# A two-layer mLSTM and RG-LRU trunk on one core: scores and gate inputs taken in wider products, row factors and gate logs moved by DMA

## The chip, the cores and the metric

One NeuronCore of a Trainium2 chip runs the whole kernel. The metric is the device time of one execution in microseconds. The engines are named as the profile names them: PE (matrix products; PEld is its weight load), DVE (vector), ACT (scalar, activations), POOL (GpSimd, which also issues DMAs of its queue) and SP (which issues most other DMAs).

## What is computed

`x` is 256 tokens by 2048 channels in float32, and there are two layers. Each layer does this, and a root-mean-square norm follows the last:

```python
u = rms_norm(x, norm_g);  p = u @ w_in          # w_in: 2048 x 12304
qk, v, o, z_a, ig, fg, xb, z_b = split(p)
q, k = split(silu(causal_dwconv(qk, qk_conv)))   # 8 heads of 128; k * 128**-0.5
i_pre = ig + i_bias;  log_f = log_sigmoid(fg + f_bias)      # 8 gate inputs each per token
h = mlstm(q, k, v, i_pre, log_f)                 # sum over s<=t of (q_t.k_s) exp(F_t-F_s+i_s-m_t) v_s
                                                 # divided by max(|the same sum of weights|, exp(-m_t))
h = layer_norm_per_head(h * sigmoid(o)) * head_norm_g
y_a = h * silu(z_a)
y_b = rg_lru(causal_dwconv(xb, lru_conv_w) + lru_conv_b, w_a, b_a, w_x, b_x, lam) * silu(z_b)
x = x + concat(y_a, y_b) @ w_out                 # w_out: 4096 x 2048
```

F is the running sum of log_f, and m the running maximum that keeps the exponentials bounded.

## The kernel before, in words

Every large product is made of three: a float32 value is split into a high part (rounded to the PE's input form) and a low part (the rest), and high by high, high by low and low by high are added in PSUM. The weights come in units of 1 MB (`raw`), in halves of 128x1024. For each half ACT casts the high part `wH` (L300), DVE subtracts to get the low part `wL` (`prepare`, L164 by its helper), and PE multiplies: 12 products of 128x128 by 128x512 (`mm_a`, L317 to L319). Four buffers each of `wH` and `wL` are in rotation, and splits are written out three halves ahead of the products (`AHEAD = 3`). Weights never stay: the program is one long stream of about 530 halves.

A layer handles four groups of two heads. A group takes the columns of qk, o, v, xb, z and zb in chunks of 8 halves each, the block-diagonal gates of the RG-LRU (`gate_half`, tile `ps_gt`) and the output products of the group before. All work on the results runs beside this stream as generators in a list `bg`. After each half `pump` gives them a budget (2.6, or 1.05 where at most two are waiting), and each `yield` takes its cost from it; `yield "wait"` lets the next generator go on, `yield None` ends the turn. `require` runs the generators until a key is set. The framework then schedules what was written for each engine, with the order as written as priority; an instruction can come well ahead of where it was written when its inputs are ready. An edge laid by hand (`order`, L208) keeps one instruction behind another.

The parts that the change touches:

- `rms_bcast` (L374). The norm factor `rstd` of each token lies with tokens on partitions. It is needed along the free axis on all partitions (`rb`). Two diagonal matrices `dg` are made on DVE from an identity, PE multiplies them by a matrix of ones (L380, `ps_rb`, plain float32), and DVE copies the result.
- `gates_mm` (L474). The 16 gate columns are laid out in a 128x104 weight `gwp` (high parts at columns 0 and 32, low parts at 64 and 96). For each of the 16 blocks of channels the high half of x (256 columns, L479) and the low half (L480) are multiplied in turn into the same 256 columns of `ps_g`.
- `gates_gen` (L483) multiplies rows of `ps_g` by `rb`, adds them, and makes the log of the forget gate, its running sum, and the running maximum on 8 partitions. `nG` goes to DRAM (L515, a POOL DMA), from where `e_gen` (L536) takes it to all partitions (`nb`, L539).
- `gates_tr` (L519) turns a 64x256 tile `sT` by two PE transposes (`ps_sT`, L527); DVE copies `aT` (L531), ACT makes `em`, the exponential (L532). `e_gen` needs `aT`, the denominators need `em`.
- In `qk_post` (L588) the scores of a head are six products by `mm3` (L560 to L562) into one bank `ps_S`: three of 256 columns and three of 128. DVE multiplies them by `E` into `Pt` in one instruction of 384 columns. Then P is split into `PH` and `PL`, and for each head and each half of the tokens P times v goes to `ps_n` (3 or 6 products of 258 columns); DVE makes denominator, `hh` and its statistics, and the turn may end after each.
- `aux` hands out the four PSUM banks that all these small products share.

Of the kernel before, what the change touches and what calls it, by code (L numbers as in the profile page):

```python
# [83 lines left out]
def tile_trunk(ctx, tc, x, xt, par, gw, gb, ws, final_g, out):  # L84
    nc = tc.nc
    V, S, G, PE = nc.vector, nc.scalar, nc.gpsimd, nc.tensor

    const = ctx.enter_context(tc.tile_pool(name="const", bufs=1))
# [64 lines left out]
    gbs = const.tile([NH, DEPTH, 2], F32, name="gbs")  # L153
    gwr = [small.tile([P, KT, 16], F32, tag="gwr", name=f"gwr{l}") for l in range(DEPTH)]

    ident = const.tile([P, P], F32, name="ident")
    make_identity(nc, ident)
    ones = const.tile([P, P], F32, name="ones")
    G.memset(ones, 1.0)
    epst = const.tile([P, 1], F32, name="epst")  # L160
    G.memset(epst, EPS)
# [46 lines left out]
    def order(ins, prev):  # L208
        tc.add_manual_dep(ins.ins, prev.ins.name,
                          mybir.DependencyInfo(mybir.DependencyClass.NoSync, mybir.DependencyReason.DATA),  # L210
                          reason="one table load for each group of functions")

    bg = deque()
    timed = []
# [89 lines left out]
    def mm_a(acc, aH, aL, k0, first, last, paired=False):  # L304
        def f(H, L):
            cols = "p (s k c) -> p k s c" if paired else "p (k c) -> p k c"
            Hv = H.rearrange(cols, k=2, **({"s": 2} if paired else {}))
            Lv = L.rearrange(cols, k=2, **({"s": 2} if paired else {}))
            a_H, a_L, ps = aH(), aL(), acc()
            for k in range(2):  # L310
                kt = k0 + k
                for t in range(2):
                    tsl = slice(P * t, P * t + P)
                    s = first and k == 0
                    e = last and k == 1
                    o = ps[:, t, :].rearrange("p (s c) -> p s c", s=2) if paired else ps[:, t, :]
                    PE.matmul(o, a_H[:, kt, tsl], Hv[:, k], start=s, stop=False)  # L317
                    PE.matmul(o, a_H[:, kt, tsl], Lv[:, k], start=False, stop=False)  # L318
                    PE.matmul(o, a_L[:, kt, tsl], Hv[:, k], start=False, stop=e)  # L319
        return f  # L320

    def mm_b(acc, k0, first, last):
# [42 lines left out]
    def rms_stats(l):  # L365
# [5 lines left out]
        V.reciprocal(out=rstd, in_=rstd)  # L371
        st["rstd", l] = rstd

    def rms_bcast(l):  # L374
        rstd = st["rstd", l]
        dg = work.tile([P, 2, P], F32, tag="sF", name="dg")
        for t in range(2):
            ts_(dg[:, t, :], ident, rstd[:, t : t + 1], ALU.mult)
        ps = aux("ps_rb")
        PE.matmul(ps[:, 0:T], ones, dg.rearrange("p t c -> p (t c)"), start=True, stop=True)  # L380
        rb = small.tile([P, T], F32, tag="rb", name="rb", bufs=1)
        V.tensor_copy(out=rb, in_=ps[:, 0:T])
        st["rb", l] = rb

    def new_ss():
# [87 lines left out]

    def gates_mm(l):  # L474
        ps = aux("ps_g")
        o = ps[0:104, 0:T]
        for kt in range(KT):
            gw_ = st["gwp"][kt // 8][:, kt % 8, :]
            PE.matmul(o, gw_, st["x"][:, kt, 0, :], start=kt == 0, stop=False)  # L479
            PE.matmul(o, gw_, st["x"][:, kt, 1, :], start=False, stop=kt == KT - 1)  # L480
        st["ps_g"] = ps

    def gates_gen(l):  # L483
        ps, rb = st["ps_g"], st["rb", l]

        scs = work.tile([P, 8, T], F32, tag="xcs", name="scs")

        def sc(nm):
            return scs[0:NH, "ifzsd".index(nm), :]

        gi, x_ = sc("i"), sc("f")
        t_ = sc("z")
        tt_(x_, ps[32:40, 0:T], rb[32:40, :], ALU.mult)
        tt_(t_, ps[96:104, 0:T], rb[96:104, :], ALU.mult)
        stt(x_, x_, gbs[:, l, 1:2], t_, ALU.add, ALU.add)
        t_ = sc("s")
        tt_(gi, ps[0:8, 0:T], rb[0:8, :], ALU.mult)
        tt_(t_, ps[64:72, 0:T], rb[64:72, :], ALU.mult)
        tt_(gi, gi, t_, ALU.add)
        yield 0.6  # L500
        q = log1p_exp_half(x_, sc)
        yield 4
        ts_(q, q, -2.0, ALU.mult)
        stt(x_, x_, 0.0, q, ALU.min, ALU.add)
        Fc = sc("z")
        V.tensor_tensor_scan(out=Fc, data0=ones[0:NH, 0:1].to_broadcast([NH, T]), data1=x_, initial=0.0, op0=ALU.mult, op1=ALU.add)
        sT = scs[0:64, 5, :]
        G.memset(sT, 0.0)
        stt(sT[0:8, :], gi, gbs[:, l, 0:1], Fc, ALU.add, ALU.subtract)
        Gm = sc("s")  # L510
        V.tensor_tensor_scan(out=Gm, data0=sT[0:8, :], data1=sT[0:8, :], initial=0.0, op0=ALU.max, op1=ALU.max)
        stt(sT[32:40, :], Fc, -1.0, Gm, ALU.mult, ALU.subtract)
        nG = sc("d")
        ts_(nG, Gm, -1.0, ALU.mult)
        nc.gpsimd.dma_start(out=nG_d[l], in_=nG)  # L515
        st["sT"] = sT
        yield 3

    def gates_tr(l):  # L519
        sT = st["sT"]  # L520
        yield None
        yield None
        for _ in range(2 + 2 * l):
            yield "wait"
        pt = aux("ps_sT")
        for t in range(2):
            PE.transpose(out=pt[:, 64 * t : 64 * t + 64], in_=sT[:, P * t : P * t + P], identity=ident[0:64, 0:64])  # L527
        ptv = pt[:, 0:128].rearrange("p (t c) -> p t c", t=2)
        aT = small.tile([P, 2, NH], F32, tag="aT", name="aT", bufs=1)
        em = small.tile([P, 2, NH], F32, tag="em", name="em", bufs=1)  # L530
        V.tensor_copy(out=aT, in_=ptv[:, :, 0:8])  # L531
        S.activation(out=em, in_=ptv[:, :, 32:40], func=AF.Exp)  # L532
        st["aT", l], st["em", l] = aT, em
        yield 0.3

    def e_gen(l, g):  # L536
        nb = small.tile([P, 2, T], F32, tag="nb", name="nb", bufs=1)
# [21 lines left out]
    def mm3(o, aH, aL, bH, bL, first=True, last=True):  # L559
        PE.matmul(o, aH, bH, start=first, stop=False)  # L560
        PE.matmul(o, aH, bL, start=False, stop=False)  # L561
        PE.matmul(o, aL, bH, start=False, stop=last)  # L562
# [25 lines left out]
    def qk_post(l, g, acc):  # L588
# [3 lines left out]
        def gen():  # L592
# [20 lines left out]
            E, em, so, (vH, vL) = st["E", l, g], st["em", l], st["so", l, g], st["v", l, g]  # L613
            Pt = work.tile([P, 2, 384], F32, tag="Pt", name="Pt")
            for h in range(2):
                ps = aux("ps_S")
                for o_, ss_, ts__ in ((0, slice(0, 128), slice(0, 256)), (256, slice(128, 256), slice(128, 256))):
                    mm3(ps[:, o_ : o_ + ts__.stop - ts__.start], q[:, 2 * h + 1, 0, ss_], q[:, 2 * h + 1, 1, ss_],
                        q[:, 2 * h, 0, ts__], q[:, 2 * h, 1, ts__])
                stt(Pt[:, h, :], ps[:, 0:384], DK_SCALE, E[:, h, :], ALU.mult, ALU.mult)  # L620
                yield 0.5
            PH = work.tile([P, 2, 384], F32R, tag="sD", name="PH")
            PL = work.tile([P, 2, 384], F32R, tag="sC", name="PL")
            S.copy(out=PH, in_=Pt)
# [4 lines left out]
            hh = work.tile([P, 2, 2, 256], F32, tag="sE", name="hh")  # L629
            mv = small.tile([P, 2, 2, 2], F32, tag="mv", name="mv", bufs=1)  # L630
            for h in range(2):
                for t in range(2):
                    pn = aux("ps_n")
                    o = pn[:, 0:258]
                    a = slice(P * t, P * t + P)
                    mm3(o, PH[:, h, a], PL[:, h, a], vH[:, 0, h, :], vL[:, 0, h, :], last=t == 0)
                    if t == 1:
                        mm3(o, PH[:, h, 256:384], PL[:, h, 256:384], vH[:, 1, h, :], vL[:, 1, h, :], first=False)
                    dn = small.tile([P, 1], F32, tag="dn", name="dn")
                    stt(dn, pn[:, 256:257], -1.0, em[:, t, 2 * g + h : 2 * g + h + 1], ALU.mult, ALU.max)  # L640
# [531 lines left out]
```

## Time and profile before

| | us |
|---|---|
| median of 3 runs (1498.24 to 1498.82) | 1498.77 |
| the profiled execution, its own time | 1498.6 |
| its span, first to last instruction | 1496.9 |
| PE busy in it | 1481.1 |
| DVE busy | 1053.3 |
| ACT busy | 916.0 |
| POOL busy | 79.2 |

Busy time counts each instruction from start to end; products overlap in the array, so the distance from one start to the next, called a slot here, says what a product costs in a dense stream. The granted TensorE clock is 0.998 of full speed on average over the span.

### The profile page before, as it was taken

The page shows a single profiled execution, that of the slowest core. Times are in us where ns is not written, and L with a number is a line of the kernel's source. Part 1 is how long each engine was busy: PE and PEld are TensorE (multiplying, and loading weights), DVE is VectorE, ACT ScalarE, POOL GpSimd, SP SyncE. Part 2 cuts the span into 40 slices and gives each one's busy share as a digit, 9 for nine tenths or more (in the row PEclk, how much of TensorE's full clock was granted, in tenths as well). Part 3 has the DMA queues.
Part 4 walks back from the last instruction along what each step waited for, and adds up shares of the span by engine and source line. Part 5 has one row for each costly group of instructions (what it writes and reads, how often), then busy time and mean ns, then how long its engine had stood idle before and what let it go on. Part 6 is the DMA issues. An engine that isn't in the chain of part 4 may idle for free.

```text
span 1496.9 us, 18541 instructions
## 1 busy us (share of the span) xinstructions
PE 1481.1 (99%) x6916; PEld 1239.3 (83%) x6916; DVE 1053.3 (70%) x1403; ACT 916.0 (61%) x1153; POOL 79.2 (5%) x138
## 2 busy tenths in 40 slices
PE   8999999999999999999999999999999999999997
PEld 6888888888888888888888888888888888888886
DVE  6777966676567855778867688766855678556794
ACT  6656855575456754558565667645855567555684
POOL 0001000000000000000000200000000000000002
PEclk9999999999999999999999999999999999999999
DMA  9766667766677666886775666568666776577773
GB/s 352 271 206 238 208 226 221 241 219 223 197 251 225 225 225 208 257 266 216 274 269 197 238 211 246 186 215 253 217 231 210 227 234 233 198 233 268 227 251 113
DMA packets 90074, 344.61 MB, mean 230 GB/s; under 512 B 9840, under 2 KB 29824, under 8 KB 67968
## 3 DMA queue, kind: packets, MB, share of 16 engines
q1 hardware_dynamic: 77888, 305.17, 58.7%
q0 software_dynamic: 9344, 33.58, 9.2%
q10 hardware_dynamic: 2752, 4.69, 0.9%
q8 instruction: 54, 0.88, 0.2%
q14 instruction: 36, 0.29, 0.1%
HBM read 306.68 MB, written 36.72 MB: 229 GB/s over the span
## 4 chain that ended last, share of the span: by engine, by line
PE 97%; DVE 1%; DMA 0%; ACT 0%; issue 0%; SPq 0%; DVEq 0%; ACTq 0%
PE acc L317 29%; PE acc L318 29%; PE acc L319 29%; PE ps_gt L724 3%; PE acc L332 3%; PE acc L955 1%; PE acc L954 1%; PE acc L956 1%; DMA raw<-in_ws_dram 0%; PE acc_x L954 0%; PE acc_x L955 0%; PE acc_x L956 0%; DVE wL L164 0%; PE ps_n L562 0%; PE ps_n L560 0%; PE ps_n L561 0%
## 5 line engine op out<-in xcount | busy, mean ns | idle before, releaser
L164 DVE TENSOR_TENSOR wL<-raw,wH 128x1024 fp32r<-128x1024 f32 (+1 forms) x526 | 636.9, 1217 | 340.3 <-ACT wH L300 340.0
L300 ACT CAST wH<-raw 128x1024 fp32r<-128x1024 f32 (+1 forms) x526 | 548.7, 1049 | 401.9 <-PE acc L319 369.8
L317 PE MATMUL acc<-wH,x_s 128*128 128x512 f32 x1472 | 574.3, 390 | 7.4 <-ACT wH L300 6.6
L318 PE MATMUL acc<-wL,x_s 128*128 128x512 f32 x1472 | 574.0, 390 | 0.4 <-DVE wL L164 0.4
L319 PE MATMUL acc<-wH,x_s 128*128 128x512 f32 x1472 | 573.2, 389 | 0.0
L317 PEld LDWEIGHTS acc<-wH,x_s 128*128 128x128 f32 x1472 | 276.7, 188 | 65.1 <-ACT wH L300 6.6
L318 PEld LDWEIGHTS acc<-wL,x_s 128*128 128x128 f32 x1472 | 276.7, 188 | 58.6 <-DVE wL L164 1.9
L319 PEld LDWEIGHTS acc<-wH,x_s 128*128 128x128 f32 x1472 | 276.7, 188 | 57.6
L317 PE MATMUL acc<-wH,yaH 128*128 128x512 f32 x224 | 87.8, 392 | 0.0
L319 PE MATMUL acc<-wH,ybL 128*128 128x512 f32 x224 | 87.4, 390 | 0.0
L319 PE MATMUL acc<-wH,yaL 128*128 128x512 f32 x224 | 87.3, 390 | 0.0
L317 PE MATMUL acc<-wH,ybH 128*128 128x512 f32 x224 | 87.2, 390 | 0.0
L318 PE MATMUL acc<-wL,ybH 128*128 128x512 f32 x224 | 87.2, 390 | 0.0
L318 PE MATMUL acc<-wL,yaH 128*128 128x512 f32 x224 | 87.2, 389 | 0.0
L429 POOL DMA_DIRECT2D fr<-moved x34 | 18.9, 555 | 724.2 <-DMA moved<-blk 426.7
L319 PEld LDWEIGHTS acc<-wH,ybL 128*128 128x128 f32 x224 | 42.0, 188 | 9.1 <-DVE ybL L164 0.3
L319 PEld LDWEIGHTS acc<-wH,yaL 128*128 128x128 f32 x224 | 42.0, 188 | 9.0
L318 PEld LDWEIGHTS acc<-wL,ybH 128*128 128x128 f32 x224 | 42.1, 188 | 8.4
L317 PEld LDWEIGHTS acc<-wH,ybH 128*128 128x128 f32 x224 | 42.0, 188 | 8.3
L318 PEld LDWEIGHTS acc<-wL,yaH 128*128 128x128 f32 x224 | 42.1, 188 | 8.2
L317 PEld LDWEIGHTS acc<-wH,yaH 128*128 128x128 f32 x224 | 42.1, 188 | 8.1
L425 DVE STREAM_TRANSPOSE blk<-tok 128x1024 f32<-128x1024 f32 x32 | 39.7, 1240 | 12.7 <-ACT tok L415 12.6
(208 smaller groups left out, 1387.5 us busy)
## 6 DMA issues: line engine op xcount, KB each, us to landing
raw<-in_ws_dram SPq DMA_DIRECT2D x172, 1024.0 KB, 5.0
raw<-in_ws_dram SPq DMA_DIRECT2D x182, 512.0 KB, 4.8
fr<-moved POOLq DMA_DIRECT2D x34, 512.0 KB, 5.8
moved<-blk SPq DMA_DIRECT2D x128, 128.0 KB, 2.3
x_d<-stage POOLq DMA_DIRECT2D x24, 512.0 KB, 5.4
x_d<-x_acc ACTq DMA_DIRECT2D x8, 512.0 KB, 7.2
x_acc<-x_d SPq DMA_DIRECT2D x8, 512.0 KB, 5.3
xp<-in_xt_dram SPq DMA_DIRECT2D x8, 256.0 KB, 7.0
```

What stands on the lines that cost most here:

```text
L164: return V.tensor_tensor(out=o, in0=a, in1=b, op=op)
L300: S.copy(out=H[:, o], in_=r[:, o])
L317: PE.matmul(o, a_H[:, kt, tsl], Hv[:, k], start=s, stop=False)
L318: PE.matmul(o, a_H[:, kt, tsl], Lv[:, k], start=False, stop=False)
L319: PE.matmul(o, a_L[:, kt, tsl], Hv[:, k], start=False, stop=e)
L332: PE.matmul(ps[:, ct, T * part : 2 * T], W[:, k, P * ct : P * ct + P], moving, start=first and k == 0 and part == 0, stop=last and k == 3 ...
L425: V.transpose(out=blk.rearrange("p m n -> p (m n)"), in_=tok.rearrange("p m c t j -> p (m c t j)"))
L429: G.dma_start(out=fr.rearrange("p a c t i -> p a (c t i)"), in_=moved)
L724: PE.matmul(o, W[:, ib, jl], xs[:, ib, a, :], start=j == 0 and i == 0 and W is Hv and a == 0, stop=i == 1 and W is Lv, skip_group_check=True)
L954: PE.matmul(o, yH[:, kt, tsl], Hv[:, k, cs], start=start and k == 0, stop=False)
L955: PE.matmul(o, yH[:, kt, tsl], Lv[:, k, cs], start=False, stop=False)
L956: PE.matmul(o, yL[:, kt, tsl], Hv[:, k, cs], start=False, stop=stop and k == 1)
```

## The change

In `gates_mm` high and low half of x are one product of 512 columns into two halves of the bank; DVE adds the halves afterwards. An edge puts the first of these products behind the last product that `mm_a` has written. The scores get a bank per block of 128 keys: one product takes high and low of q at once against the high part of k, a second adds low of k by high of q; DVE multiplies both halves by E (E is overwritten) and adds. P times v is written for both halves of the tokens of a head before the DVE work on either. The norm factor goes to DRAM and back to all partitions by two POOL DMAs, and `sT` is turned by a DVE transpose in blocks of 32x32 and eight POOL DMAs; the exponential and the key for E come two waits later. The identity and the matrix of ones go.

```diff
     def rms_bcast(l):
-        rstd = st["rstd", l]
-        dg = work.tile([P, 2, P], F32, tag="sF", name="dg")
-        for t in range(2):
-            ts_(dg[:, t, :], ident, rstd[:, t : t + 1], ALU.mult)
-        ps = aux("ps_rb")
-        PE.matmul(ps[:, 0:T], ones, dg.rearrange("p t c -> p (t c)"), start=True, stop=True)
         rb = small.tile([P, T], F32, tag="rb", name="rb", bufs=1)
-        V.tensor_copy(out=rb, in_=ps[:, 0:T])
+        G.dma_start(out=rb_d[l].rearrange("t p -> p t"), in_=st["rstd", l])
+        G.dma_start(out=rb, in_=rb_d[l].rearrange("t p -> (t p)").partition_broadcast(P))
...
     def gates_mm(l):
-            PE.matmul(o, gw_, st["x"][:, kt, 0, :], start=kt == 0, stop=False)
-            PE.matmul(o, gw_, st["x"][:, kt, 1, :], start=False, stop=kt == KT - 1)
+            m = PE.matmul(ps[0:104, :], st["gwp"][kt // 8][:, kt % 8, :], st["x"][:, kt].rearrange("p a t -> p (a t)"),
+                          start=kt == 0, stop=kt == KT - 1)
+            if kt == 0:
+                order(m, st["mm"])
...
     gates_gen:
-        tt_(x_, ps[32:40, 0:T], rb[32:40, :], ALU.mult)
+        tt_(x_, ps[32:40, T : 2 * T], rb[32:40, :], ALU.mult)
+        tt_(gi, ps[32:40, 0:T], rb[32:40, :], ALU.mult)
+        tt_(x_, x_, gi, ALU.add)
...
-        tt_(t_, ps[64:72, 0:T], rb[64:72, :], ALU.mult)
-        tt_(gi, gi, t_, ALU.add)
+        for rows, half in ((slice(0, 8), slice(T, 2 * T)), (slice(64, 72), slice(0, T))):
+            tt_(t_, ps[rows, half], rb[rows, :], ALU.mult)
+            tt_(gi, gi, t_, ALU.add)
...
     gates_tr:
-        pt = aux("ps_sT")
-        for t in range(2):
-            PE.transpose(out=pt[:, 64 * t : 64 * t + 64], in_=sT[:, P * t : P * t + P], identity=ident[0:64, 0:64])
-        V.tensor_copy(out=aT, in_=ptv[:, :, 0:8])
-        S.activation(out=em, in_=ptv[:, :, 32:40], func=AF.Exp)
+        V.transpose(out=sb, in_=sT)
+        for q_ in range(2):
+            for a in range(4):
+                rows = slice(32 * a, 32 * a + 32)
+                G.dma_start(out=at[q_][rows], in_=sv[32 * q_ : 32 * q_ + 32, :, a, 0:NH])
         yield 0.3
+        for _ in range(2):
+            yield "wait"
+        S.activation(out=at[1], in_=at[1], func=AF.Exp)
+        st["aT", l], st["em", l] = at
...
     scores, for h in range(2):
+                for b in range(2):
+                    n_ = T - P * b
+                    ps, ss_, ts__ = aux("ps_S"), slice(P * b, P * b + P), slice(P * b, T)
+                    both = ps[:, 0 : 2 * n_].rearrange("p (a t) -> p a t", a=2)
+                    PE.matmul(both, q[:, 2 * h + 1, 0, ss_], q[:, 2 * h, :, ts__], start=True, stop=False, ...)
+                    PE.matmul(ps[:, 0:n_], q[:, 2 * h + 1, 1, ss_], q[:, 2 * h, 0, ts__], start=False, stop=True, ...)
+                    stt(Pt[:, h, part], ps[:, n_ : 2 * n_], DK_SCALE, E[:, h, part], ALU.mult, ALU.mult)
+                    stt(E[:, h, part], ps[:, 0:n_], DK_SCALE, E[:, h, part], ALU.mult, ALU.mult)
+                tt_(Pt[:, h, :], Pt[:, h, :], E[:, h, :], ALU.add)
+                yield 1.0
...
     P times v, for h in range(2):
+                pns = []
                 for t in range(2):
-                    pn = aux("ps_n")
-                    o = pn[:, 0:258]
+                    pns.append(aux("ps_n"))
+                    o = pns[t][:, 0:258]
...
+                for t in range(2):
+                    pn = pns[t]
```

## Rows read from the trace of the kernel before

**Rows 1.** The page's first part: busy time, share of the span, count.
```profile
PE 1481.1 (99%) x6916; PEld 1239.3 (83%) x6916; DVE 1053.3 (70%) x1403; ACT 916.0 (61%) x1153; POOL 79.2 (5%) x138
```

**Rows 2.** Waits: who waited for whom, us in total, times, longest.
```profile
PE acc L317 <- DVE x_acc L164: 0.8, 1, 0.8
...
ACT wH L300 <- PE acc L319: 369.8, 263, 2.4
```

**Rows 3.** Timeline of PE, scores of a group: start us, us, engine, line, instruction.
```profile
111.15 0.39 PE L317 MATMUL acc<-wH,x_s 128*128 128x512 f32 x1
...
112.51 0.28 PE L560 MATMUL ps_S<-qks 128*128 128x256 f32 x1
...
112.87 0.23 PE L560 MATMUL ps_S<-qks 128*128 128x128 f32 x1
...
113.83 0.45 PE L317 MATMUL acc<-wH,x_s 128*128 128x512 f32 x1
114.11 0.39 PE L318 MATMUL acc<-wL,x_s 128*128 128x512 f32 x1
```

**Rows 4.** Timelines of DVE and PE: gate inputs in layer 0, norm factor in layer 1.
```profile
45.80 0.17 DVE L371 RECIPROCAL rstd<-rstd 128x2 f32<-128x2 f32 x1 [0.38 <-ACT rstd L370]
...
45.99 0.28 PE L479 MATMUL ps_g<-x_s,gwp 128*104 128x256 f32 x1
...
47.88 0.59 PE L380 MATMUL ps_rb<-dg,ones 128*128 128x256 f32 x2
...
793.15 0.40 PE L319 MATMUL acc<-wH,x_s 128*128 128x512 f32 x1
...
794.05 0.40 PE L318 MATMUL acc<-wL,x_s 128*128 128x512 f32 x1
```

**Rows 5.** Timeline of PE around the two transposes of layer 0.
```profile
73.29 0.39 PE L319 MATMUL acc<-wH,x_s 128*128 128x512 f32 x1
...
74.21 0.39 PE L318 MATMUL acc<-wL,x_s 128*128 128x512 f32 x1
```

**Rows 6.** Timeline of PE: 12 weight products behind a P piece, two such stretches.
```profile
129.66 0.39 PE L317 MATMUL acc<-wH,x_s 128*128 128x512 f32 x1
...
132.41 0.39 PE L317 MATMUL acc<-wH,x_s 128*128 128x512 f32 x1
...
232.27 0.40 PE L317 MATMUL acc<-wH,yaH 128*128 128x512 f32 x1
...
235.05 0.28 PE L560 MATMUL ps_n<-vH,PH 128*128 128x258 f32 x1
```

**Rows 7.** Timelines of POOL, DVE and ACT: gate logs until E, layer 0.
```profile
72.70 0.53 POOL L515 DMA_DIRECT2D nG_d<-scs  x1 [7.61 <-DVE scs L171]
...
82.15 1.01 DVE L172 TENSOR_SCALAR E<-nb,aT 128x256 f32<-128x256 f32 x4 [5.16 <-DMA nb<-nG_d]
...
83.19 0.85 ACT L551 ACTIVATE E<-E 128x768 f32<-128x768 f32 x1 [5.20 <-DVE E L172]
```

**Rows 8.** Timeline of PE, some five halves later.
```profile
95.87 0.39 PE L317 MATMUL acc<-wH,x_s 128*128 128x512 f32 x1
96.27 0.50 PE L318 MATMUL acc<-wL,x_s 128*128 128x512 f32 x1
```

**Rows 9.** Groups by line and form: busy us, mean ns of one, idle before.
```profile
L164 DVE TENSOR_TENSOR wL<-raw,wH 128x1024 fp32r<-128x1024 f32 x522 | 634.1, 1221 | 338.0 <-ACT wH L300 337.8
...
L300 ACT CAST wH<-raw 128x1024 fp32r<-128x1024 f32 x522 | 546.2, 1052 | 399.8 <-PE acc L319 369.8 <-DMA raw<-in_ws_dram 6.2 <-issue 5.2
...
L167 DVE SCALAR_TENSOR_TENSOR hh<-ps_n,dn,so 128x256 f32<-128x256 f32 x32 | 15.3, 479 | 0.3
...
L167 DVE SCALAR_TENSOR_TENSOR Pt<-ps_S,E 128x384 f32<-128x384 f32 x16 | 8.7, 545 | 5.6 <-PE ps_S L562 5.6
...
L164 DVE TENSOR_TENSOR scs<-ps_g,rb 8x256 f32<-8x256 f32 x8 | 3.3, 417 | 1.9 <-PE ps_g L480 1.8
```

**Rows 10.** DMA issues: engine, count, size, median us from issue to landing.
```profile
x_acc<-in_x_dram SPq DMA_DIRECT2D x4, 512.0 KB, 8.2
```

More of the change, by code (lines that the diff above doesn't have):

```diff
@@ L6 @@
 from concourse import mybir
-from concourse.masks import make_identity
 from concourse._compat import with_exitstack
@@ L154, in tile_trunk @@
     gwr = [small.tile([P, KT, 16], F32, tag="gwr", name=f"gwr{l}") for l in range(DEPTH)]
-    ident = const.tile([P, P], F32, name="ident")
-    make_identity(nc, ident)
-    ones = const.tile([P, P], F32, name="ones")
+    ones = const.tile([NH, 1], F32, name="ones")
     G.memset(ones, 1.0)
@@ L210, in order @@
                           mybir.DependencyInfo(mybir.DependencyClass.NoSync, mybir.DependencyReason.DATA),
-                          reason="one table load for each group of functions")
+                          reason="an order of the program")
     bg = deque()
@@ L318, in f @@
                     PE.matmul(o, a_H[:, kt, tsl], Lv[:, k], start=False, stop=False)
-                    PE.matmul(o, a_L[:, kt, tsl], Hv[:, k], start=False, stop=e)
+                    st["mm"] = PE.matmul(o, a_L[:, kt, tsl], Hv[:, k], start=False, stop=e)
         return f
@@ L372, in rms_stats @@
         st["rstd", l] = rstd
+    rb_d = [dram.tile([2, P], F32, name=f"rb_d{l}") for l in range(DEPTH)]
     def rms_bcast(l):
-        rstd = st["rstd", l]
-        dg = work.tile([P, 2, P], F32, tag="sF", name="dg")
-        for t in range(2):
-            ts_(dg[:, t, :], ident, rstd[:, t : t + 1], ALU.mult)
-        ps = aux("ps_rb")
-        PE.matmul(ps[:, 0:T], ones, dg.rearrange("p t c -> p (t c)"), start=True, stop=True)
         rb = small.tile([P, T], F32, tag="rb", name="rb", bufs=1)
-        V.tensor_copy(out=rb, in_=ps[:, 0:T])
+        G.dma_start(out=rb_d[l].rearrange("t p -> p t"), in_=st["rstd", l])
+        G.dma_start(out=rb, in_=rb_d[l].rearrange("t p -> (t p)").partition_broadcast(P))
         st["rb", l] = rb
@@ L475, in gates_mm @@
         ps = aux("ps_g")
-        o = ps[0:104, 0:T]
         for kt in range(KT):
-            gw_ = st["gwp"][kt // 8][:, kt % 8, :]
-            PE.matmul(o, gw_, st["x"][:, kt, 0, :], start=kt == 0, stop=False)
-            PE.matmul(o, gw_, st["x"][:, kt, 1, :], start=False, stop=kt == KT - 1)
+            m = PE.matmul(ps[0:104, :], st["gwp"][kt // 8][:, kt % 8, :], st["x"][:, kt].rearrange("p a t -> p (a t)"),
+                          start=kt == 0, stop=kt == KT - 1)
+            if kt == 0:
+                order(m, st["mm"])
         st["ps_g"] = ps
@@ L505, in gates_gen @@
         Fc = sc("z")
-        V.tensor_tensor_scan(out=Fc, data0=ones[0:NH, 0:1].to_broadcast([NH, T]), data1=x_, initial=0.0, op0=ALU.mult, op1=ALU.add)
+        V.tensor_tensor_scan(out=Fc, data0=ones.to_broadcast([NH, T]), data1=x_, initial=0.0, op0=ALU.mult, op1=ALU.add)
         sT = scs[0:64, 5, :]
@@ L515, in gates_gen @@
         nc.gpsimd.dma_start(out=nG_d[l], in_=nG)
-        st["sT"] = sT
+        st["sT"], st["sb"] = sT, scs[0:64, 6, :]
         yield 3
@@ L524, in gates_tr @@
             yield "wait"
-        pt = aux("ps_sT")
-        for t in range(2):
-            PE.transpose(out=pt[:, 64 * t : 64 * t + 64], in_=sT[:, P * t : P * t + P], identity=ident[0:64, 0:64])
-        ptv = pt[:, 0:128].rearrange("p (t c) -> p t c", t=2)
-        aT = small.tile([P, 2, NH], F32, tag="aT", name="aT", bufs=1)
-        em = small.tile([P, 2, NH], F32, tag="em", name="em", bufs=1)
-        V.tensor_copy(out=aT, in_=ptv[:, :, 0:8])
-        S.activation(out=em, in_=ptv[:, :, 32:40], func=AF.Exp)
-        st["aT", l], st["em", l] = aT, em
+        sb = st["sb"]
+        V.transpose(out=sb, in_=sT)
+        sv = sb.rearrange("p (t a i) -> p t a i", t=2, a=4)
+        at = [small.tile([P, 2, NH], F32, tag=f"at{q_}", name=f"at{q_}", bufs=1) for q_ in range(2)]
+        for q_ in range(2):
+            for a in range(4):
+                rows = slice(32 * a, 32 * a + 32)
+                G.dma_start(out=at[q_][rows], in_=sv[32 * q_ : 32 * q_ + 32, :, a, 0:NH])
         yield 0.3
+        for _ in range(2):
+            yield "wait"
+        S.activation(out=at[1], in_=at[1], func=AF.Exp)
+        st["aT", l], st["em", l] = at
     def e_gen(l, g):
@@ L615, in gen @@
             for h in range(2):
[L616 to L621, printed above, removed]
+                for b in range(2):
+                    n_ = T - P * b
+                    ps, ss_, ts__ = aux("ps_S"), slice(P * b, P * b + P), slice(P * b, T)
+                    both = ps[:, 0 : 2 * n_].rearrange("p (a t) -> p a t", a=2)
+                    PE.matmul(both, q[:, 2 * h + 1, 0, ss_], q[:, 2 * h, :, ts__], start=True, stop=False,
+                              skip_group_check=True)
+                    PE.matmul(ps[:, 0:n_], q[:, 2 * h + 1, 1, ss_], q[:, 2 * h, 0, ts__], start=False, stop=True,
+                              skip_group_check=True)
+                    part = slice(T * b, T * b + n_)
+                    stt(Pt[:, h, part], ps[:, n_ : 2 * n_], DK_SCALE, E[:, h, part], ALU.mult, ALU.mult)
+                    stt(E[:, h, part], ps[:, 0:n_], DK_SCALE, E[:, h, part], ALU.mult, ALU.mult)
+                tt_(Pt[:, h, :], Pt[:, h, :], E[:, h, :], ALU.add)
+                yield 1.0
             PH = work.tile([P, 2, 384], F32R, tag="sD", name="PH")
```

## The prediction

> **What bounds the kernel now.** I read the busy times first: PE is busy for 1481.1 of 1496.9 us, DVE for 70%, ACT for 61% [rows 1]. Busy alone proves little, so the waits come next. In the whole list PE waits for another engine's result behind its start only in a few places below 1 us; the largest is 0.8 us at the layer boundary [rows 2]. The other way round ACT waits 369.8 us, in 263 pieces, for PE to free a weight buffer [rows 2]. So this is a stream of products with everything else running ahead of it, and an edit is worth what it takes out of PE's dense sequence, less whatever new wait breaks through to PE.
>
> How far ahead is the rest? A split can start when PE has freed one of four buffers; PE then has three halves before it needs it. A half is 12 slots of 512 columns. Six of them, from 111.15 to 112.51, take 1.36 us [rows 3], so a slot is 0.227 and a half 2.72. Three halves are 8.2 us, cast and subtraction take 1.05 and 1.22 [rows 9], so ACT or DVE may stand still for about 5.9 us before PE stops. This is the cover on which everything below rests.
>
> **The change part by part.**
>
> *Scores.* From the first score product at 112.51 to the second weight product at 114.11 are 1.60 us; less one slot of 0.227 the 12 products of a group cost 1.373 [rows 3]. Three of 256 columns take 0.36 (112.51 to 112.87), 0.118 to 0.12 each; the remaining six of 128 columns take (1.373 - 6 x 0.118) / 6 = 0.111, nearly as much for half the columns. Their price is set by something per product, not by columns (there is a weight load with each). After: per head one of 512, two of 256, one of 128: 0.227 + 2 x 0.118 + 0.111 = 0.574, two heads 1.148. Saved 0.225 a group, eight groups 1.80 us. Bounds: the columns streamed are equal before and after (1152 a head), so if columns alone counted the saving would be 0; above, 12 x 0.12 - 1.148 would be 0.29 a group, 2.3.
>
> *Gate inputs.* 16 products of 256 columns take 1.89 us from 45.99 to 47.88 [rows 4], 0.118 each. 32 of them become 16 of 0.227: 3.78 - 3.63 = 0.15 a layer, 0.3 in all; between 0 and 0.3 by the same argument. The edge moves them behind one more half, on the same engine: nothing gained or lost there, since PE is dense on both sides.
>
> The Trainium skill, "TensorE: Matmul & The Clock Gate", section "Back-to-back issue gap", gives a warm product N/2.4 + 2.5 ns, which is 109 for 256 columns and 216 for 512 where the rows above show 118 and 227; by it the fixed part that merging saves is 2.5 ns, not 9. By the page the gate inputs would be worth an estimated 0.08 us instead of 0.3. I keep the rows.
>
> *Norm factor.* From 793.15 to 794.05 are 0.90 us with two weight slots in it [rows 4]: 0.45 for the two plain float32 products with their changeover. Twice: 0.9 us removed.
>
> *Transposes.* 73.29 to 74.21 is 0.92, less two slots: 0.466 [rows 5]. Twice 0.93. Both are nothing at the least only if other work had to fill PE there, and PE has weight products waiting in either place.
>
> *P products in one piece.* Their number and width stay. After a split piece the next 12 weight products take 2.78 us (232.27 to 235.05), after a joined one 2.75 (129.66 to 132.41), against 2.72 undisturbed [rows 6]. There are two changeovers fewer a group in six of eight groups (the first group of each layer already runs joined): at 0.03 each 0.4 us; between 0 and 0.7 (0.06 each).
>
> Sum: 1.80 + 0.30 + 0.90 + 0.93 + 0.40 = 4.3 us off PE.
>
> *What is added on DVE.* Per head four multiplications (two of 256 columns at 0.48 [rows 9], two of 128, at most the same) and a sum (as the 0.545 now) replace one of 0.545: at most 1.9 us more, 3.8 a group, 31 in all on an engine with 440 us free. In a group's score step this comes at once, and ACT waits with the cast of P behind it, with the casts of `wH` queued behind that on ACT. 3.8 is inside the 5.9, so I cost it at 0; without that cover it would be up to 3.8 a group. The gates get four more operations of 0.42 [rows 9], 1.7 us a layer, while copies and the diagonal go: 0.
>
> *The wait for rb.* Two DMAs in a chain now stand between `rstd` and the gate operations. The only such chain in the trace, `nG` to DRAM and back to `nb`, takes 9.45 us from issue at 72.70 to the first E at 82.15 [rows 7]. `rstd` is done at 45.97 [rows 4], so the factor is there at about 55.4. Gate products that start at 45.99 as now end at 49.6 (16 slots of 0.227); one half later, as the edge has it, at 52.3. DVE stands 3.1 to 5.8 us at its first gate operation, with splits `wL` queued behind it; against 5.9. Between 0 and, with six operations of 0.42 on top before the next split, 2.4 us of PE in a layer; I take 0, since the edge puts the need later.
>
> *The wait for the gate logs.* E now waits for `nb` until 82.15; DVE stands 5.16 us, ACT 5.20 behind it [rows 7]. This eats the cover: PE still loses 0.17 us at 95.87, where a slot takes 0.40 [rows 8]. After the change eight POOL issues of 0.53 [rows 7], 4.2 us, share the queue with `nb`, and an exponential on ACT waits for the last of them with `wH` casts queued behind it. If they go ahead of `nb`, `nb` lands about 1 us later than now; if behind, the last lands at 77.4 + 0.5 + 4.2 + 4.2 = 86.3 (half of the 9.45 chain a DMA), 4 us later. The need is written two halves, 5.4 us, later. So between -0.2 and +4 us a layer; I take +0.2 for both together, near the present loss, because the later need and the later landing about cancel.
>
> The Trainium skill, "DMA: Bandwidth & Descriptors", section "Anatomy of one DMA — SWDGE (gpsimd) path", gives a POOL DMA about 2.0 us fixed; the chain above shows 4.7 for each of two. By the page rb would be there an estimated 4 us after `rstd`, both new waits would end before their need, and the sum would be the full 4.3. The same page, "Rules for kernel authors", says that a run that is not contiguous becomes a descriptor per element, which speaks against the 4-byte runs of the norm factor; no row here shows such a DMA.
>
> The start and the layer boundary (its 0.8 us waits for `x_acc`) hold none of the edits. Net 4.3 - 0.2 = 4.1 us. The profiled execution took 1498.6, 0.17 below the median: 1498.6 - 4.1 = 1494.5 there, 1494.7 against the median.
>
> **The rivals.**
>
> *Part is given back (1497).* One of the new waits breaks through by 1.5 to 3 us in one layer, or by about 1 in each. For it: the present wait of 5.2 is already at the edge of 5.9, and PE does lose there. Against: elsewhere in the chunk PE never stops, and the need is put later. 1498.8 - 4.3 + 2.5 = 1497.
>
> *Only columns count (1496.6).* The score and gate savings are 0, and 0.90 + 0.93 + 0.40 remain: 1498.8 - 2.2. Against: the slots of 128 columns at 0.111.
>
> *Slower (1506).* The exponential of the gate logs is taken up by ACT where it stands now, half a microsecond behind 74.21 [rows 5], because the scheduler expects the DMAs sooner than they come, as it evidently did with E (both engines stood over 5 us). Landing at 86.3, ACT stands 11.6 us, 5.7 beyond the cover, in each layer: 11.4 - 4.3 = 7 us slower. With landings of 8.2 instead of 4.2 [rows 10] it is 15 slower. It decides from a stand of about 9.5 us in each layer (5.9 + 3.7). Against: it is written two halves later, and 86.3 is the late end.
>
> **How the numbers follow.** About 0.2%, 3 us, is what a measurement can tell from no change. Forecast (1493.8 to 1495.7): 0.54. Part given back: 0.28, hardly any of it beyond 3 us faster. Only columns: 0.08, within 3 us. Slower: 0.10. Faster by over 0.2% gets the forecast and 0.03 of the second: 0.57; within 0.2%: 0.33; slower 0.10. The range from 1493.5 (all upper bounds at PE, 5.3 us) to 1499.5 leaves out the slower case and little more.
>
> **What would show it.** Right: `ps_rb` and `ps_sT` gone from PE; the 8 score products of a group in 1.15 us from first to the weight slot; gate products 0.227 apart; no new line in PE's waits. Wrong: PE waiting for `wH` or `wL` within 15 us of the gate operations or of E, which would show as slots far above 0.227 behind an ACT stand at the exponential; score slots of 512 columns plus two of 256 that add up to 1.37 as now. Losses of PE at every group's scores would mean that DVE's extra 3.8 us are not covered.

## The result and the profile after

| | before | after |
|---|---|---|
| median, us (runs, spread) | 1498.88 (6, 1498.24 to 1499.43) | 1505.49 (6, 1504.49 to 1508.11) |
| ratio, 95% interval | | 1.0046, 1.0036 to 1.0056 |
| profiled execution, us (span) | 1498.6 (1496.9) | 1505.33 (1503.6) |

The change made the kernel slower by 0.46%, 6.6 us, against a forecast of 4.1 us faster and a range that ended at 1499.5. What the change was to take out of PE did go. One new wait took the place of it, at one spot of layer 0.

The page's first part after, to be read against [rows 1]. PE has 72 products fewer, and is as busy as before: busy says nothing here of the 6.7 us.
```profile
PE 1481.2 (99%) x6844; PEld 1236.3 (82%) x6844; DVE 1066.8 (71%) x1469; ACT 914.2 (61%) x1154; POOL 81.1 (5%) x156
```

PE's waits after, all of them (us in total, times, longest). The second line is the start of the program, and the third is that of [rows 2].
```profile
PE acc L315 <- DVE wL L161: 6.7, 3, 4.7
PE acc L314 <- ACT wH L297: 6.6, 1, 6.6
PE acc L314 <- DVE x_acc L161: 0.8, 1, 0.8
```
Before, the counterpart of the first line (L315 is L318 there) is 0.4 us, at the start of the program:
```profile
PE acc L318 <- DVE wL L164: 0.4, 1, 0.4
```

**The savings are there.** The scores of a group on PE's timeline: from the first product at 121.53 to the second weight product at 122.92 are 1.39 us, less a slot of 0.227 1.16, where [rows 3] gave 1.373.
```profile
121.53 0.39 PE L620 MATMUL ps_S<-qks 128*128 128x512 f32 x1
...
122.58 0.22 PE L622 MATMUL ps_S<-qks 128*128 128x128 f32 x1
122.63 0.45 PE L314 MATMUL acc<-wH,x_s 128*128 128x512 f32 x1
122.92 0.39 PE L315 MATMUL acc<-wL,x_s 128*128 128x512 f32 x1
```

Summed over the whole span, the busy time of the score products (a row of the table by windows, for the tile `ps_S` alone; the span, then PE, PEld and DVE busy with their counts, clock, DMA share, GB/s), first before, then after: 1.75 us less on PE, and 11 us more for DVE's reads of the scores, at which PE stops nowhere.
```profile
0.00:1503.60 1503.60, 11.85 (x96) 12.18 (x96) 8.71 (x16) 1.00 0.69 229
```
```profile
0.00:1503.60 1503.60, 10.10 (x64) 9.71 (x64) 19.67 (x64) 1.00 0.70 229
```

**Where the time went.** The chain of waits after (start, length, what), around the norm factor of layer 0. The store of `rstd` takes 9.40 us, the load of `rb` 4.82: from issue to the first gate operation 14.6 us, where the chain of [rows 7] gave 9.45.
```profile
47.76 9.40 DMA rb_d<-rstd
57.16 0.30 issue
57.46 4.82 DMA rb<-rb_d
62.37 0.75 DVE scs L161 x2
...
64.02 1.13 DVE wL L161
```

DVE's timeline there (`x3` at the end of a row is three operations in a row). The first gate operation stands in DVE's order right behind the split that ends at 52.95. It waits for 9.42 us, and the next split, for which PE stops, comes only behind it and three more operations, at 63.95.
```profile
51.73 1.23 DVE L161 TENSOR_TENSOR wL<-raw,wH 128x1024 fp32r<-128x1024 f32 x1 [2.29 <-ACT wH L297]
62.37 1.21 DVE L161 TENSOR_TENSOR scs<-ps_g,rb 8x256 f32<-8x256 f32 x3 [9.42 <-DMA rb<-rb_d]
63.61 0.41 DVE L161 TENSOR_TENSOR scs<-scs 8x256 f32<-8x256 f32 x1
63.95 1.21 DVE L161 TENSOR_TENSOR wL<-raw,wH 128x1024 fp32r<-128x1024 f32 x1
```

The edge did not put the need later. The gate products start at 45.48, where they started at 45.99 before [rows 4], and are through at 49.35; DVE comes to its gate operation only at 52.95 because a split, whose cast it had to wait for, stands ahead of it.
```profile
45.48 3.87 PE L471 MATMUL ps_g<-x_s,gwp 128*104 128x512 f32 x16
```

ACT stands too, for 9.43 us at the first activation of the gates, with casts behind it. PE's stop doesn't come from there: the halves of the splits at 63.95 and 66.92 had been cast before it, at 52.14 and 54.91.
```profile
66.69 0.42 ACT L175 ACTIVATE scs<-scs 8x256 f32<-8x256 f32 x1 [9.43 <-DVE scs L164]
```

PE's timeline: the slot of the product at 60.10 is 5.11 us long, and the slots behind it are 0.43 instead of 0.227 until 70.50.
```profile
60.10 0.39 PE L314 MATMUL acc<-wH,x_s 128*128 128x512 f32 x1
65.21 0.80 PE L315 MATMUL acc<-wL,x_s 128*128 128x512 f32 x1 [4.72 <-DVE wL L161]
65.80 0.63 PE L316 MATMUL acc<-wH,x_s 128*128 128x512 f32 x1
...
70.50 0.50 PE L315 MATMUL acc<-wL,x_s 128*128 128x512 f32 x1
70.83 0.39 PE L316 MATMUL acc<-wH,x_s 128*128 128x512 f32 x1
```

The table by windows for PE (stretch, its length, PE busy with its count, granted clock, DMA share, GB/s) says why: over the 5.3 us behind the stop the clock is granted at 0.50, the lower of its two levels (1.2 of 2.4 GHz). The mean of 0.87 over the stop says that it fell while PE stood. Before the stop it is full, and in the last stretch nearly so, at 0.98.
```profile
52.00:60.00 8.00, 8.00 (x37) 1.00 0.70 109
60.00:65.20 5.20, 0.49 (x3) 0.87 0.18 37
65.20:70.50 5.30, 5.29 (x13) 0.50 0.51 198
70.50:76.00 5.50, 5.50 (x24) 0.98 0.62 128
```

The stop costs 5.11 - 0.23 = 4.88 us. The 13 slots from 65.21 to 70.83 take 5.62 instead of 13 x 0.227 = 2.95, 2.67 more. Together 7.55 us, more than everything that the change saves. Another 0.3 us goes between 73.1 and 75.9, so the step in the ledger below is 7.9.

In layer 1 the same chain is longer (11.3 us until the store releases `rb`) and costs nothing: POOL issues it at 772.66 and 784.69, and DVE's first gate operation at 807.70 waits for its products alone.
```profile
772.66 0.73 POOL L375 DMA_DIRECT2D rb_d<-rstd  x1 [3.08 <-DVE rstd L368]
784.69 0.56 POOL L376 DMA_DIRECT2D rb<-rb_d  x1 [11.29 <-DMA rb_d<-rstd]
```
```profile
807.70 1.21 DVE L161 TENSOR_TENSOR scs<-ps_g,rb 8x256 f32<-8x256 f32 x3 [1.39 <-PE ps_g L471]
```

The gate logs cost a little in both layers. In layer 0 E now waits for `at`, 3.65 us (in [rows 7] 5.16, for `nb`), and PE's slot from 95.16 to 97.00 is 1.6 us too long, where [rows 8] has 0.17. In layer 1 a slot at 845.61 is 0.7 too long.
```profile
93.53 1.01 DVE L169 TENSOR_SCALAR E<-nb,at 128x256 f32<-128x256 f32 x4 [3.65 <-DMA at<-scs]
```
```profile
95.16 0.39 PE L314 MATMUL acc<-wH,x_s 128*128 128x512 f32 x1
97.00 0.50 PE L315 MATMUL acc<-wL,x_s 128*128 128x512 f32 x1 [1.45 <-DVE wL L161]
```

**The ledger.** Both kernels have the same 6220 weight products in the same sequence, so the start of each after, less its start before, gives a lag, and its steps show where time was lost or won (worked out from both PE timelines, us):

| place | step of the lag |
|---|---|
| start of the program, clock rises some slots later | +0.7 |
| gate inputs and norm factor, layer 0 | -0.5 |
| the stop at 60.1 and the slow slots behind it | +7.9 |
| transposes, layer 0 | -0.5 |
| E, layer 0 | +1.6 |
| scores and pieces, layer 0 | -1.2 |
| norm factor, gate inputs, transposes, layer 1 | -1.1 |
| E, layer 1 | +0.7 |
| scores and pieces, layer 1, and the layer boundary | -1.1 |
| behind the last weight product | +0.3 |
| sum, against 1503.6 - 1496.9 = 6.7 | +6.8 |

The savings add up to 4.4 us, against a forecast of 4.3; 0.2 of them lie at the layer boundary, where no edit stands. Among them the gate inputs are half of what was forecast: 16 products from 45.48 to 49.19 take 3.71 us, 0.232 each and not 0.227, against 32 x 0.118 = 3.78 before, so 0.07 a layer where 0.15 stood.

### The profile page after: what moved, and what is told of

It is laid out like the page before. It is cut to its first block, busy times and chain, and to the rows that moved or that the text cites. A ratio compares the mean times of both kernels' runs of the same rounds, so it can differ in the third digit from the quotient of the medians.

```text
span 1503.6 us, 18518 instructions
## 1 busy us (share of the span) xinstructions
PE 1481.2 (99%) x6844; PEld 1236.3 (82%) x6844; DVE 1066.8 (71%) x1469; ACT 914.2 (61%) x1154; POOL 81.1 (5%) x156
## 4 chain that ended last, share of the span: by engine, by line
PE 91%; DMA 4%; DVE 3%; ACT 1%; issue 1%; POOL 0%; SPq 0%; ACTq 0%; DVEq 0%
PE acc L315 27%; PE acc L314 27%; PE acc L316 27%; PE ps_gt L734 3%; PE acc L329 3%; DMA raw<-in_ws_dram 3%; DVE wL L161 1%; DMA rb_d<-rstd 1%; PE acc L966 1%; PE acc L964 1%; PE acc L965 1%; PE acc_x L966 0%; PE acc_x L964 0%; PE acc_x L965 0%; PE ps_S L620 0%
## 5 line engine op out<-in xcount | busy, mean ns | idle before, releaser
L315 PE MATMUL acc<-wL,x_s 128*128 128x512 f32 x1472 | 575.8, 391 | 6.8 <-DVE wL L161 6.7
L315 PEld LDWEIGHTS acc<-wL,x_s 128*128 128x128 f32 x1472 | 277.6, 189 | 66.9 <-DVE wL L161 10.0
L315 PE MATMUL acc<-wL,ybH 128*128 128x512 f32 x224 | 87.2, 389 | 0.0
L315 PE MATMUL acc<-wL,yaH 128*128 128x512 f32 x224 | 87.2, 389 | 0.0
L315 PEld LDWEIGHTS acc<-wL,ybH 128*128 128x128 f32 x224 | 42.1, 188 | 8.5
L315 PEld LDWEIGHTS acc<-wL,yaH 128*128 128x128 f32 x224 | 42.1, 188 | 8.2
```

## The experiments

The lag that is told with each is against the profile of before, at the same product.

**1. The norm factor by PE again.** The change with this one part undone.
```diff
 def rms_bcast(l):
+    dg = work.tile([P, 2, P], F32, tag="sF", name="dg")
...
+    PE.matmul(ps[:, 0:T], ones, dg.rearrange("p t c -> p (t c)"), start=True, stop=True)
...
-    G.dma_start(out=rb_d[l].rearrange("t p -> p t"), in_=st["rstd", l])
-    G.dma_start(out=rb, in_=rb_d[l].rearrange("t p -> (t p)").partition_broadcast(P))
+    V.tensor_copy(out=rb, in_=ps[:, 0:T])
```


> The changed kernel with the norm factor by PE again, all else as changed. Theory A (the stand of DVE for the norm factor in layer 0 costs about 8.4 us of PE, and its removal from PE gives 0.9 back): 1505.5 - 8.4 + 0.9 = 1498.0, no PE stop near 60 us. Rival B (the loss comes from E and the gate logs, or from DVE's extra work on the scores): stays above 1503. Rival C (the edge that holds the gate products back makes the stop): stays above 1503, the stop near 60 us remains.

Measured: 1496.78 us (11 runs), 0.9984 of before (0.9975 to 0.9993). The first gate operation runs at 49.47 instead of 62.37, the stop at 60 is gone, and the median is 8.7 us below that of the change, 1.2 more than the first theory had. PE's waits:
```profile
PE acc L317 <- ACT wH L300: 6.6, 1, 6.6
PE acc L317 <- DVE x_acc L164: 0.8, 1, 0.8
PE acc L318 <- DVE wL L164: 0.7, 1, 0.7
```
The norm factor by DMA is what made the change slower; the rest of it is faster than before.

**2. The norm factor by DMA alone.** The kernel before with `rms_bcast` of the change, nothing else.
```diff
 def rms_bcast(l):
-    PE.matmul(ps[:, 0:T], ones, dg.rearrange("p t c -> p (t c)"), start=True, stop=True)
...
-    V.tensor_copy(out=rb, in_=ps[:, 0:T])
+    G.dma_start(out=rb_d[l].rearrange("t p -> p t"), in_=st["rstd", l])
+    G.dma_start(out=rb, in_=rb_d[l].rearrange("t p -> (t p)").partition_broadcast(P))
```


> The kernel before with the norm factor by the two DMAs alone. A: 1498.9 + 8.4 - 0.9 = 1506.4 or more, because the gate products are over earlier here and DVE stands at least as long; PE stops near 60 us in layer 0 and not in layer 1. B and C: within 1 us of 1498.9, or 0.9 below.

Measured: 1507.83 us (5 runs), 1.0057 (1.0045 to 1.007): 9 us slower alone. DVE's timeline, then PE's, show the same place as in the change, with a longer stop and the slow slots behind it:
```profile
62.43 1.30 DVE L164 TENSOR_TENSOR scs<-ps_g,rb 8x256 f32<-8x256 f32 x3 [9.56 <-DMA rb<-rb_d]
```
```profile
66.54 0.79 PE L318 MATMUL acc<-wL,x_s 128*128 128x512 f32 x1 [6.19 <-DVE wL L164]
```

**3. The three edits of PE's products alone** (scores, gate inputs with their edge, pieces); norm factor and gate logs by PE.
```diff
 def gates_tr(l):
-    V.transpose(out=sb, in_=sT)
...
-            G.dma_start(out=at[q_][rows], in_=sv[32 * q_ : 32 * q_ + 32, :, a, 0:NH])
+        PE.transpose(out=pt[:, 64 * t : 64 * t + 64], in_=sT[:, P * t : P * t + P], identity=ident[0:64, 0:64])
...
+    S.activation(out=em, in_=ptv[:, :, 32:40], func=AF.Exp)
```
(and `rms_bcast` as in the first experiment)

> Scores, gate products with their edge, and P products as changed; norm factor and gate logs by PE as before. If the slots add up as forecast: 1.8 + 0.3 + 0.4 = 2.5 us off, 1496.4. If DVE's extra work on the scores breaks through: not below 1498.9. If only columns counted: 1498.5.

Measured: 1498.58 us (11 runs), 0.9993 (0.9985 to 1.0002): a miss, only 0.5 us below before. The savings per group of heads are in the trace in full; against them stand 0.9 us at the start of the program, 0.15 at the gate inputs and the norm factor of layer 0, 0.7 behind E in layer 0, and 1.0 at the product from 902.73 to 903.97 in layer 1. PE's waits for DVE:
```profile
PE acc L318 <- DVE wL L164: 2.5, 3, 1.2
```

**4. The gate logs by DVE's turn and DMAs alone.** The kernel before with `gates_tr` of the change.
```diff
 def gates_tr(l):
-        PE.transpose(out=pt[:, 64 * t : 64 * t + 64], in_=sT[:, P * t : P * t + P], identity=ident[0:64, 0:64])
...
+    V.transpose(out=sb, in_=sT)
...
+            G.dma_start(out=at[q_][rows], in_=sv[32 * q_ : 32 * q_ + 32, :, a, 0:NH])
```


> The kernel before with the gate logs turned on DVE and by eight DMAs alone. A alone says nothing of it; from the lag of PE in the changed kernel the two stops behind E cost 1.7 and 0.8 us and the transposes give 1.0 back: 1498.9 + 1.5 = 1500.4, with PE stops 10 to 15 us behind the first E in both layers. If those stops are a follow-up of the stop for the norm factor: 1498.9 - 1.0 = 1497.9.

Measured: 1498.86 us (11 runs), 0.9997 (0.9988 to 1.0006): no change, and neither of the two times that were expected. The lag drops by 0.5 where the transposes of layer 0 were, rises by 1.25 behind E, where DVE now waits for `at`, and drops by 0.5 in layer 1.
```profile
82.66 0.55 DVE L172 TENSOR_SCALAR E<-nb,at 128x256 f32<-128x256 f32 x2 [4.97 <-DMA at<-scs]
```
What it saves on PE, one wait gives back.

**5. The factor stored in runs of 128 bytes.** In the change, DVE turns the factor first and four DMAs store it, instead of 256 runs of 4 bytes.
```diff
-    G.dma_start(out=rb_d[l].rearrange("t p -> p t"), in_=st["rstd", l])
+    V.tensor_copy(out=rp[:, 0:2], in_=st["rstd", l])
+    V.transpose(out=rq, in_=rp)
+    for b in range(4):
+        G.dma_start(out=rb_d[l][:, 32 * b : 32 * b + 32], in_=rq[32 * b : 32 * b + 2, :])
```


> The changed kernel; the norm factor is first turned on DVE in blocks of 32x32, so that its store goes out in four POOL DMAs with runs of 128 bytes instead of one with 256 runs of 4 bytes. Theory R (the runs make the store slow, 9.4 and 11.7 us to landing): each store lands in 3 to 4.5 us as nG does, the factor is there about 11 us behind rstd instead of 14.6, DVE stands about 6 us, at the edge of the 5.9 us cover: 1497 to 1499. Rival Q (the POOL queue or the crowded DMA engines at that moment make it slow): the stores land in 8 us or more, no gain, 1505 or above.

Measured: 1504.01 us (5 runs), 1.0031 (1.002 to 1.0043), between the two theories. The chain of waits:
```profile
48.19 1.73 POOL rb_d L381 x3
49.91 4.75 DMA rb_d<-rq
...
55.23 5.49 DMA rb<-rb_d
60.74 0.75 DVE scs L161 x2
```
A store lands in 2.2 to 4.8 us instead of 9.4 to 11.7, so the runs are a good part of its price. But the turn and the issues of four DMAs eat much of that, and the gate operations begin only 1.6 us earlier. PE still stops twice, for 1.2 us until 63.58 and for 3.55 until 70.53, and pays the slow slots. The second stop is not DVE's stand any more. In DVE's order 5.9 us of gate operations and a turn of another tile stand without a gap between two splits, and the cast for the second of them came late, at 65.39, behind ACT's stand at the gates.
```profile
62.32 1.20 DVE L161 TENSOR_TENSOR wL<-raw,wH 128x1024 fp32r<-128x1024 f32 x1
...
69.32 1.15 DVE L161 TENSOR_TENSOR wL<-raw,wH 128x1024 fp32r<-128x1024 f32 x1
```
```profile
65.06 0.42 ACT L175 ACTIVATE scs<-scs 8x256 f32<-8x256 f32 x1 [5.72 <-DVE scs L164]
```

**6. The store from ACT's queue.**
```diff
-    G.dma_start(out=rb_d[l].rearrange("t p -> p t"), in_=st["rstd", l])
+    S.dma_start(out=rb_d[l].rearrange("t p -> p t"), in_=st["rstd", l])
```


> The changed kernel with the store of the norm factor (256 runs of 4 bytes) issued from ACT's queue instead of POOL's. Theory R: the store still takes 8 to 11 us, 1504 to 1506. Rival Q, if it is POOL's queue: it lands in 3 to 5 us, DVE stands 5 us less, 1498.

Measured: 1501.73 us (12 runs, 1496.81 to 1504.58), 1.0015 (1.0007 to 1.0024), between the two theories. In the profiled run the store takes 7.73 instead of 9.40 and the load 6.66 instead of 4.82, so the gate operations begin at 62.47, no earlier than in the change. PE stops for 2.34 us all the same, half as long, because one split more runs ahead of the standing operation:
```profile
52.01 2.36 DVE L161 TENSOR_TENSOR wL<-raw,wH 128x1024 fp32r<-128x1024 f32 x2 [2.29 <-ACT wH L297]
62.47 1.21 DVE L161 TENSOR_TENSOR scs<-ps_g,rb 8x256 f32<-8x256 f32 x3 [8.10 <-DMA rb<-rb_d]
```
So the queue isn't shown to matter. What shows is that the place of the waiting operation among the splits counts, which the next run tries on purpose.

**7. The gate operations later in DVE's order.** In the change, written four halves later and held behind the splits written until then.
```diff
+            st["wl"] = tt_(L[:, o], r[:, o], H.bitcast(F32)[:, o], ALU.subtract)
...
-        tt_(x_, ps[32:40, T : 2 * T], rb[32:40, :], ALU.mult)
+        late(tt_(x_, ps[32:40, T : 2 * T], rb[32:40, :], ALU.mult))
...
-            yield None
+            for _ in range(5):
+                yield None
```


> The changed kernel with the same two DMAs; the gate operations that need the norm factor are written four halves later and held on DVE behind the splits written till then. If what costs is DVE standing in order at the factor with splits queued behind it, and not the DMA as such: no stop near 60 us, no drop of the clock, 1505.5 - 8.4 = 1497.1. If the transfers disturb the weight loads or the gate log chain is too late for the scores: 1500 or above.

Measured: 1508.91 us (6 runs), 1.0055 (1.0043 to 1.0067). The stop at 60 us is gone as meant: the first gate operation stands for 0.49 us at 64.28 and the lag is -1.0 until 97. But all that follows the gates comes later too. Of the gate logs' chain POOL issues the first store at 90.95 instead of 85.12, E stands until 101.24, ACT's exponential behind it until 102.03 with the casts of `wH` behind that, and PE stops at 100.6 for 4.6 us, at 169.5 for 1.0, and in layer 1 between 878 and 888 for 2.7 in three waits, the longest 2.0.
```profile
102.03 1.28 ACT L538 ACT_TABLE_LOAD   x1 [5.32 <-DMA at<-scs]
...
104.18 2.92 ACT L297 CAST wH<-raw 128x1024 fp32r<-128x1024 f32 x3
```
The wait moved down the chain, and cost as much there. The edit moves ACT's activation of the gates along with the operations on DVE (its stand is 0.94 us here), so it doesn't part the two; that DVE alone made the stop of the change is read from the rows above and from experiment 6.

**8. As 7, and E one half later too.**
```diff
-        for _ in range(2):
+        for _ in range(3):
             yield "wait"
...
+                if g == 0:
+                    order(e, wl)
```


> The norm factor by DMA with its gate operations put later on DVE (as in the run before it) and, in addition, the E operations of a layer's first group one half later, behind the splits written until then. Theory A (only operations that stand in order ahead of splits cost; the chain itself may be 14.6 us long): no PE slot above 0.45 us between 55 and 110 us, PE's waits for wL and wH below 1 us a place, and 1494.7 to 1496. Theory B (with the factor by DMA the gate logs come too late for the first scores, whatever the order): a PE stop of 2 us or more at the scores of group 0 or at the products behind them, with a clock drop behind it, and 1500 or more.

Measured: 1511.77 us (5 runs), 1.0077 (1.0065 to 1.009): the second theory. PE stops for 5.5 us at the same place, and again in layer 1 from 910.8, for 2.6 and 1.0 us, where the lag goes from 8.0 to 13.7 with the slow slots behind the stop. On ACT:
```profile
103.19 1.28 ACT L538 ACT_TABLE_LOAD   x1 [5.19 <-DMA at<-scs]
```
With the factor this late, holding E back a little doesn't help: the DMAs behind the gates end at 101 to 103 us, and the casts are still queued behind what waits for them.

**9. The factor by PE, and E one half later.** The first experiment with the edit of the eighth.
```diff
-        for _ in range(2):
+        for _ in range(3):
             yield "wait"
...
+            for e in (ts_(E[:, h, 0:256], nb[:, h, :], aT[:, 0, hd : hd + 1], ALU.add, 0.0, ALU.min),
+                      ts_(E[:, h, 256:384], nb[:, h, 128:256], aT[:, 1, hd : hd + 1], ALU.add, 0.0, ALU.min)):
+                if g == 0:
+                    order(e, wl)
```


> Norm factor by PE, all else as changed (1496.8 in its own run), and the E operations of the first group of each layer held on DVE behind the splits written till then, one half later. If the loss of 0.7 us behind the first E (slots near 88 us) comes from DVE and ACT standing at E: it goes, 1496.1. If those stands are covered anyway: 1496.8, no change.

Measured: 1495.52 us (10 runs, 1494.58 to 1496.95), 0.9977 (0.9968 to 0.9986): faster than both kernels, and 1.3 us below the first experiment in the median, though the spreads overlap (1495.19 to 1498.09 there). E stands for nothing on DVE, and PE waits for a split 0.2 us in all:
```profile
86.65 1.00 DVE L172 TENSOR_SCALAR E<-nb,at 128x256 f32<-128x256 f32 x4
```
```profile
PE acc L318 <- DVE wL L164: 0.2, 1, 0.2
```

**10. As 3, and E three halves later than it is written there.**
```diff
+        for _ in range(3 if g == 0 else 0):
+            yield "wait"
...
+                if g == 0:
+                    order(e, wl)
```


> Scores, gate inputs with the edge, and pieces changed; norm factor and gate logs by PE as before; the E operations of a layer's first group three halves later than they are written before, and behind the splits written until then. Theory A (E standing in DVE's order ahead of splits is a cost of its own, 0.7 to 1.6 us in a layer, whoever brings the gate logs): it is faster than the same kernel without the hold (1498.6) by 1 to 2 us, 1496.6 to 1497.6, which with the 1.8 us of the two PE steps still in it (0.90 for the factor, 0.93 for the transposes) lies 1 to 2 us above the version that has the gate logs by DMA and the same hold (1495.5). Theory B (E's stand is nothing but noise at the start of the program): within 0.5 us of 1498.6.

Measured: 1497.69 us (11 runs), 0.9992 (0.9983 to 1.0001). Against the third, 0.9 us less in the median, between the two theories: the spreads overlap (1496.85 to 1499.31, 1496.76 to 1499.16). The profile is clearer: E stands for nothing now, and one wait for a split is left, before the product at 902.36 in layer 1.
```profile
PE acc L318 <- DVE wL L164: 0.9, 1, 0.9
```
There ACT has a table load and eight activations in a row ahead of a cast (895.31 to 899.82). They run at the time of before, while PE has become 1.5 us earlier, so the wait gives 1.0 of them back. In the ninth ACT begins that row 2.8 us sooner and PE loses nothing. Why ACT's order differs there was not tried.

## Why the prediction was wrong

- **The products: right.** 4.2 us measured, the layer boundary apart, against 4.3. The score products are 1.75 us less of busy PE (1.80 forecast), with 1.16 us a group (1.148). That only columns count is refuted. The gate inputs were put too high: the slot of 0.227 was taken from the weight products, theirs is 0.232, and 0.15 us is left of 0.30.
- **DVE's added work at the scores: right.** 11 us more on DVE for reading the scores, and PE waits at no group's scores.
- **The wait for `rb`: the step that failed.** It was taken as 0, between 0 and 2.4 us a layer, with the reason that the edge puts the need later. It cost 7.6 us in layer 0, and 0 in layer 1. What was off in it, and what was not:
  - The chain's length was taken from the one row at hand, 9.45 us, and is 14.6; the store of 256 runs of 4 bytes takes 9.4 and 11.7. The prediction quoted the rule that speaks against such runs (the Trainium skill, "DMA: Bandwidth & Descriptors", section "Rules for kernel authors") and didn't price it. The runs agree with it: 2.2 to 4.8 us a store in runs of 128 bytes, turn and issues apart.
  - The same page's fixed part of about 2.0 us a POOL DMA, in the section "Anatomy of one DMA — SWDGE (gpsimd) path", doesn't hold for this chain: 9.40 and 4.82, for 1 KB and 128 KB.
  - DVE's stand was put at 3.1 to 5.8 us, from 49.6 or 52.3 to 55.4, and was 9.4, from 52.95 to 62.37. That the start came near 52.3 is luck: the edge did not move the gate products, which were through at 49.35, and a split ahead in DVE's order set the start. Of the 7.0 us at its end 5.2 are the chain's length, and 1.8 that POOL issues the store at 47.76, where `rstd` was taken at 45.97. The cover itself was right: from 52.95 to the next split at 63.95 are 11.0 us, and 11.0 less the 4.9 of the stop leaves 6.1, against 5.9.
- **What a stop costs beyond its length: not in the sum.** Every rival priced a stop by its length. Behind this one the 13 slots at the lower clock cost 2.67 us, over half as much again. The shorter stops behind E show none of it.
- **The wait for the gate logs: right in kind, small in size.** -0.2 to +4 us a layer was the range, +0.2 for both waits the value taken; measured 1.6 and 0.7. Alone it cancels the transposes (experiment 4), and with E placed later the median is 1.3 us lower with spreads that overlap (experiment 9), and 0.9 lower in experiment 10, which is not clear of noise.
- **The slower rival: nearly the size, not the place.** It said 1506, through ACT standing at the exponential of the gate logs in each layer. The change lost its time 30 us earlier, on DVE, in one layer. The rival's mechanism is real: it is what experiments 7 and 8 ran into.

That the norm factor by DMA is the cause is shown (experiments 1 and 2). That the place of its first user in DVE's order carries the stop is read from DVE's rows and borne out by 6, where the gate operations begin as late as in the change and one split more ahead of them halves the stop; in 7 the stop went although the chain was longer (16.2 us, from 48.10 to 64.25), but ACT's activation was moved with it. Not tried: holding the gate operations back by less than four halves, which might find a place between the two stops; the chain from issue to E suggests little room. The 0.7 us at the start, where the clock rises some slots earlier or later from one program to the next, stays unexplained.

## What to carry to other kernels

Moving a small result from the dense engine to DMA trades a certain half microsecond for a chain of two DMAs; price it by rows with the same run length, and take the bound from the longest one seen. What matters then is not when the result is needed but what is queued behind the operation that waits for it: look where it stands in its engine's order, and how much of the dense engine's supply lies behind it. And a stop of the dense engine is priced with the slow slots that follow it, or not at all.

## What the runs showed of the hardware

- A POOL DMA that stores 1 KB as 256 runs of 4 bytes took 9.4 and 11.7 us to land in the change, and 8.7 to 11.2 in experiments 2, 7 and 8; 256 bytes as two runs of 128 took 2.2 to 4.8 (experiment 5). From ACT's queue the first form took 7.7 and 11.7 (experiment 6).
- With a stop of 4.9 us the granted clock went from 1.00 to 0.50, and for 5.3 us behind it the slots of 512 columns from 0.227 to 0.427. The clock was at 0.50 as well behind the stops of 3.6, 4.6, 5.5 and 6.2 us (experiments 5, 7, 8 and 2); after the one of 2.3 (experiment 6) the clock was at 0.57 over 66 to 70 us; after those of 1.6 and 0.7 behind E the clock was 1.00, and the slots 0.23 from the second on.
